# Loads placed ahead, and the heads' stores and small norm transfers moved from SyncE's queue to GpSimd's, in a hybrid SSD layer

## The chip, the cores and the metric

The kernel runs on one core of one Trainium2 chip. The metric is device microseconds of one execution. The core's engines are TensorE (PE, matmuls), VectorE (DVE), ScalarE (ACT), GpSimd (POOL) and SyncE (SP, which here only issues transfers); each works through its own list of instructions in order, and they wait for each other by semaphores. Times before the change: 1659.56, 1663.52 and 1663.94 us, median 1663.52.

## The reference, cut to what matters

One layer on a sequence of 2048 tokens of width 1024, fp32. `rmsnorm`, `silu`, `softplus` and the causal convolution `causal_dwconv` are as usual.

```python
h = rmsnorm(x, norm_pre)
xbc, dt_raw, z_ssd, sc_h, sc_b, sc_c, z_sc = split(h @ w_in)
xbc = silu(causal_dwconv(xbc, ssd_conv_w, ssd_conv_b))        # xs, bm, cm
dt, a = softplus(dt_raw + dt_bias), -exp(a_log)
# ssd_chunked: 16 heads of 64, 2 groups, state 64, chunks of 128
cb      = einsum("bclgn,bcsgn->bgcls", cc, bc)
y_diag  = einsum("bgrcls,bcsgrp->bclgrp", cb * decay_in, xd)
states  = einsum("bclgn,bclgrp->bcgrpn", bc, xd * decay_states)
# prev_states: states carried over the chunks, zero ahead of the first
y_off   = einsum("bclgn,bcgrpn->bclgrp", cc, prev_states) * decay_out
y       = y_diag + y_off + d_skip * xs
y_ssd   = grouped_rmsnorm(y * silu(z_ssd), ssd_norm)           # 2 groups
y_sc    = sc_b * causal_dwconv(sc_c * sc_h, sc_conv_w) * silu(z_sc)
x = x + rmsnorm(concat(y_ssd, y_sc) @ w_out, norm_post)
return x + sigmoid(x @ w_ple_gate) * (p @ w_ple_proj)
```

## The kernel before

All large products run as three matmuls of fp32 values that are split into a rounded half and its remainder (ACT casts, DVE subtracts). The input projection and the last gate product use seven sub-products (Strassen-Winograd). The sequence is cut in two blocks b of 1024 tokens and four groups of 512.

The stages, by the profile: to 50 us the per-layer embeddings; 50 to 570 the input projection of block 0, 570 to 1030 that of block 1; to about 1306 the heads; then the output projection (tiles `mo`) to about 1490, and the gate product (`mg`) to 1653.

*Under block 1's projection* `later_weights()` makes split halves of later weights: it loads rows `A_g` and `A_o`, and `keep` casts (ACT, L542), subtracts (DVE, L543) and stores them (SP, L544) to `sg_d` and `so_d`. Among ACT's other work there are copies of the projection's sums out of PSUM (L326), which free banks for PE.

*The heads* go in pairs j = 0 to 3 for each block. A pair loads xs, the rows `m` of accumulated decay (L1035) and the gate rows gz; ACT makes exponentials of m (L1003 for `ea`, L1040 for the mask m), DVE multiplies m with the products `gsb` (L1043), carries the states `sprev` from chunk to chunk (L1027) and forms `ea` (L1030); PE adds, in `py`, ea times sprev and m times xd. The result is gated on DVE (L1071, L1072) and stored to `yz_d` (L1073), and its squares are summed in `ssum`. `begin()` and `step_g` do what a block needs once: loads of `ct` and `bt` (L944, L946), their product (`pg`), which ACT copies to `gsb` (L961) and GpSimd masks (L963, the page's AFFINE_SELECT).

Between the heads' steps PE works on a filler, `under()`: the half of the output projection that reads the short convolution's rows (`os`, L817). Its sums go through `po` (ACT, L918) to `part_d` (SP, L919). The filler also makes the split rows of coming token groups: loads `mraw`, casts (L215) and subtracts (L216).

After a block's last pair `inv_rms` makes the group norm: a matmul over ssum (`pn`), a copy (L244), four stores of a row to `grs_d` (L246), a load of them in columns, `pn_q` (L249), a square root and a reciprocal (L251), and a store back (L252). The broadcast load `gn` of this (L856) is then used to make the rows of the output projection.

In the output projection DVE's L1180 adds a sum `mo` in PSUM to the stored part (load `part`), into `x2`; the second norm's small transfers are at L1200 and L1202. `second(tg, unit, at, lag)` adds the residual rows `xres`, which are loaded `lag` units before.

What sets the order: a scheduler places each engine's instructions at build time by its own cost estimates; matmuls of the heads and the filler stay in program order. Every transfer waits for the eighth before it of its kind of queue. Tiles come from pools that are opened and closed like a stack: a tile in a pool that lies where a closed pool lay waits for all that used that place.

## Time and profile before

| | |
|---|---|
| runs | 1659.56, 1663.52, 1663.94 us, median 1663.52 |
| profiled execution, own time | 1660.71 us |
| its span, first to last instruction | 1659.0 us |
| mean granted TensorE clock | 0.997 |
| PE busy | 1634.0 us (98%) |
| DVE, ACT, POOL busy | 1273.4 (77%), 805.7 (49%), 69.3 us (4%) |
| transfers | 314.73 MB, all of the program's issued on SP |

PE's busy time counts from the modelled start to the modelled end of a matmul. A line of a timeline gives a start, a duration, the engine and line, and a number of like instructions; in brackets stands how long the engine was idle before and what ended that. For a transfer, the time is that of its issue on SP (SPq), not of the data.

### The profile page before, as it was taken

How to read it: one execution, taken by the hardware profiler on the slowest of the kernel's cores; microseconds unless marked ns; L12 is line 12 of the kernel's file. 1: busy time of each engine (PE TensorE's matmuls, PEld its weight loads, DVE VectorE, ACT ScalarE, POOL GpSimd, SP SyncE). 2: the span in 40 equal slices, each digit the busy share in tenths (PEclk: the TensorE clock that was granted, in tenths of full speed). 3: DMA queues.
4: the chain of work that ended last, by engine and by line, in shares of the span. 5: the costliest groups of instructions: out<-in, count | busy, mean ns of one | idle time of the engine just before them, and what ended most of it. 6: DMA issues, size and time to landing. Idle time of an engine off the chain costs nothing.

```text
span 1659.0 us, 22821 instructions
## 1 busy us (share of the span) xinstructions
PE 1634.0 (98%) x8296; PEld 1344.2 (81%) x8296; DVE 1273.4 (77%) x1913; ACT 805.7 (49%) x1450; POOL 69.3 (4%) x79
## 2 busy tenths in 40 slices
PE   9999999999999999999999999999999999999998
PEld 8888888888888888788888888888788788888776
DVE  6998777987769999877768678478777747687785
ACT  8663444434337555543435345466667424234342
POOL 0000000000000311000000001000100000000000
PEclk9999999999999999999999999999999999999999
DMA  9352322774216478951323227788788635547996
GB/s 324 140 197 83 101 94 82 258 242 142 72 64 219 178 269 283 298 172 64 108 64 107 71 66 266 254 303 292 278 288 293 202 113 180 160 160 253 323 309 218
DMA packets 135557, 314.73 MB, mean 190 GB/s; under 512 B 18698, under 2 KB 20234, under 8 KB 135444
## 3 DMA queue, kind: packets, MB, share of 16 engines
q1 hardware_dynamic: 135444, 313.27, 55.3%
q8 instruction: 65, 1.06, 0.3%
q14 instruction: 48, 0.39, 0.1%
HBM read 221.81 MB, written 91.41 MB: 189 GB/s over the span
## 4 chain that ended last, share of the span: by engine, by line
PE 74%; DVE 10%; DMA 9%; ACT 4%; issue 2%; SPq 0%; DVEq 0%; ACTq 0%
PE mo L226 10%; PE mg_X L1278 4%; PE mg_Y L1278 4%; PE os L817 3%; PE A_ple L226 2%; DMA m<-acs_d 2%; ACT m L1040 1%; PE A_xs1X L322 1%; PE A_gc6X L322 1%; PE A_gb7X L322 1%; PE A_gb5X L322 1%; PE A_gc7X L322 1%; PE A_z3X L322 1%; PE A_xs3X L322 1%; PE A_gb6X L322 1%
## 5 line engine op out<-in xcount | busy, mean ns | idle before, releaser
L817 PE MATMUL os<-act_m,ws_os 128*128 128x512 f32 x768 | 184.6, 397 | 0.7 <-ACT A_z L749 0.7
L226 PE MATMUL mo<-act_m,ws_o 128*128 128x512 f32 x768 | 179.3, 394 | 3.5 <-DVE x L1180 3.3
L226 PEld LDWEIGHTS mo<-act_m,ws_o 128*128 128x128 f32 x768 | 144.0, 189 | 37.8 <-DVE x L1180 6.0
L817 PEld LDWEIGHTS os<-act_m,ws_os 128*128 128x128 f32 x768 | 142.9, 189 | 34.6 <-issue 4.2
L1278 PE MATMUL mg_X<-act_x2s,ws_g 128*128 128x512 f32 x384 | 90.8, 393 | 0.7 <-ACT gth L1249 0.7
L147 DVE TENSOR_TENSOR ws_A_gb<-wr_A_gb,ws_A_gb 128x512 fp32r<-128x512 f32 x96 | 65.7, 684 | 27.1 <-ACT ws_A_gb L146 27.1
L1278 PEld LDWEIGHTS mg_X<-act_x2s,ws_g 128*128 128x128 f32 x384 | 70.8, 188 | 18.6 <-ACT gth L1249 1.7
L146 ACT CAST ws_A_gc<-wr_A_gc 128x512 fp32r<-128x512 f32 x96 | 59.7, 622 | 49.7 <-PE A_gc5X L322 8.3
L146 ACT CAST ws_A_gb<-wr_A_gb 128x512 fp32r<-128x512 f32 x96 | 59.7, 622 | 48.4 <-issue 5.0
L668 DVE SCALAR_TENSOR_TENSOR xo<-ux,cols,xo 128x1024 f32<-128x1024 f32 x60 | 76.6, 1280 | 5.3 <-ACT xo L664 4.2
L1040 ACT ACTIVATE m<-m,adt 128x128 f32<-128x128 f32 x256 | 79.8, 390 | 0.5
L147 DVE TENSOR_TENSOR ws_A_gc<-wr_A_gc,ws_A_gc 128x512 fp32r<-128x512 f32 x96 | 65.8, 685 | 12.2 <-ACT ws_A_gc L146 11.4
L1278 PE MATMUL mg_Y<-act_x2s,ws_g 128*128 128x512 f32 x288 | 68.1, 392 | 1.7 <-DVE kp L1251 1.2
L1278 PEld LDWEIGHTS mg_Y<-act_x2s,ws_g 128*128 128x128 f32 x288 | 53.5, 188 | 14.7 <-DVE kp L1251 2.4
L1043 DVE SCALAR_TENSOR_TENSOR m<-m,gsb 128x1024 f32<-128x1024 f32 x32 | 39.5, 1247 | 28.2 <-ACT m L1040 20.0
L1180 DVE TENSOR_TENSOR x<-mo,part 128x512 f32<-128x512 f32 x32 | 22.1, 689 | 47.4 <-PE mo L226 42.4
L1185 ACT ACTIVATE sq<-x 128x512 f32<-128x512 f32 x28 | 17.7, 633 | 70.5 <-DVE x L1180 70.4
L146 ACT CAST ws_A_z<-wr_A_z 128x512 fp32r<-128x512 f32 x48 | 29.9, 623 | 40.9 <-DVE wr_A_z L199 13.9
L215 ACT CAST act_m<-mraw 128x512 fp32r<-128x512 f32 x64 | 37.5, 620 | 23.8 <-DMA mraw<-ysc_d 9.6
L146 ACT CAST ws_A_xs<-wr_A_xs 128x512 fp32r<-128x512 f32 x48 | 29.9, 623 | 36.6 <-issue 11.6
L226 PE MATMUL A_ple<-act_p,ws_p 128*128 128x512 f32 x192 | 45.8, 396 | 0.1
L147 DVE TENSOR_TENSOR ws_A_z<-wr_A_z,ws_A_z 128x512 fp32r<-128x512 f32 x48 | 32.9, 685 | 16.6 <-ACT ws_A_z L146 16.5
(521 smaller groups left out, 3742.7 us busy)
## 6 DMA issues: line engine op xcount, KB each, us to landing
ws_g<-sg_d SPq DMA_DIRECT2D x56, 512.0 KB, 5.0
wr_A_gc<-in_w_t_dram SPq DMA_DIRECT2D x64, 256.0 KB, 2.7
wr_A_gb<-in_w_t_dram SPq DMA_DIRECT2D x64, 256.0 KB, 3.0
ws_os<-so_d SPq DMA_DIRECT2D x32, 512.0 KB, 5.7
m<-acs_d SPq DMA_DIRECT2D x32, 512.0 KB, 6.4
sg_d<-A_gs SPq DMA_DIRECT2D x28, 512.0 KB, 4.3
ple_d<-A_pe SPq DMA_DIRECT2D x32, 256.0 KB, 3.9
wr_A_xs<-in_w_t_dram SPq DMA_DIRECT2D x32, 256.0 KB, 3.0
```

Of the source, the lines that this page charges most:

```text
L146: S.copy(sp[:, 0, :kn, :], raw[:, :kn, :])
L147: V.tensor_tensor(sp[:, 1, :kn, :], raw[:, :kn, :], sp[:, 0, :kn, :].bitcast(F32), ALU.subtract)
L215: S.copy(a[:, 0, :], src)
L226: TE.matmul(out, sp[:, a, (k0 + k) % 4, :], act[k0 + k][:, b, :], start=k0 + k == 0 and q == 0, stop=k0 + k == n - 1 and q == 2)
L322: TE.matmul(out, sp[:, a, k % 4, :], t[:, b, ts_], start=p in OPENS and k == 0 and q == 0, stop=k == nk - 1 and q == 2, skip_group_check=True)
L668: V.scalar_tensor_tensor(o, u[:, q:q + TB], col(w0 + q), o, ALU.mult, ALU.add)
L817: inst = f(*a, **k)
L1040: S.activation(m[:, c, :], m[:, c, :], AF.Exp, bias=nacs[b][:, h, c:c + 1])
L1043: V.scalar_tensor_tensor(mf, mf, 1.0, s["gsb"][gr], ALU.min, ALU.mult)
L1180: evac.append(V.tensor_tensor(x2[d], ps[:, i, :], pt[:, i, :], ALU.add))
L1185: S.activation(sq, x2[d], AF.Square)
L1278: TE.matmul(out, sp[:, a, k, :], ops_[t, p][k][:, b, :], start=p in OPENS and m_ == 0, stop=m_ == 11, skip_group_check=True)
```

## The change

- `later_weights` issues the loads of A_o three ahead of the `keep` that uses them.
- GpSimd's queue, not SP's, issues the 32 stores to `part_d`, the 16 stores to `yz_d`, the heads' norms' small transfers (parameter `by` of `inv_rms`) and the second norms' store and broadcast load, 68 transfers in all.
- The first chunk's state is no longer written out: block 0 copies the first sums from PSUM and leaves out the products with the zero state, block 1 reads `carry` in place. GpSimd's memsets and copies go.
- The rows of token group 2 are loaded one at a time and earlier (`load_raw`, `mix_tile`), and the mixing of groups 3 and 0 is spaced otherwise.
- `ct`, `gsb` and `btok` get a pool of their own below `per`; x2's tiles get one (`px`) that is opened first, below the part loads. x2 so lies where the heads' working tiles (po and others, `t4`) lay, and the part loads where ct, gsb and btok lay.
- `second(2, ...)` and `second(3, ...)` get lags of 3 and 4 units, from 2.

```diff
-    def inv_rms(row_d, accs, eps, name, banks, scale=1.0):
+    def inv_rms(row_d, accs, eps, name, banks, scale=1.0, by=nc.sync):
-            nc.sync.dma_start(row_d.rearrange("a (g t) -> (a g) t", t=TG)[g:g + 1, :], row[32 * g:32 * g + 1, :])
+            by.dma_start(row_d.rearrange("a (g t) -> (a g) t", t=TG)[g:g + 1, :], row[32 * g:32 * g + 1, :])
-        nc.sync.dma_start(q, col_d)
+        by.dma_start(q, col_d)
-        nc.sync.dma_start(col_d, q)
+        by.dma_start(col_d, q)
...
-            for d in range(KD):
-                for q in range(2):
-                    w = A.ph.tile([P, TG], F32, tag="h2", name=f"A_o{d}_{q}")
-                    nc.sync.dma_start(w.rearrange("p (k c) -> p k c", c=P), w_o[d, :, 4 * (q + 2):4 * (q + 2) + 4, :])
-                    keep(so_d[d][q], w, f"A_os{d}_{q}")
+            ahead = []
+            for n in range(2 * KD + 3):
+                if n < 2 * KD:
+                    d, q = divmod(n, 2)
+                    ahead.append(A.ph.tile([P, TG], F32, tag="h2", name=f"A_o{d}_{q}"))
+                    nc.sync.dma_start(ahead[n].rearrange("p (k c) -> p k c", c=P),
+                                      w_o[d, :, 4 * (q + 2):4 * (q + 2) + 4, :])
+                if n >= 3:
+                    d, q = divmod(n - 3, 2)
+                    keep(so_d[d][q], ahead[n - 3], f"A_os{d}_{q}")
                     yield
...
+        pg_ = st.enter_context(tc.tile_pool(name="pg", bufs=1))
         per = st.enter_context(tc.tile_pool(name="per", bufs=1))
...
+            def load_raw(tg, k):
+                t = praw.tile([P, 4, P], F32, tag="wraw", name=f"mraw_{tg}_{KD + k}").rearrange("p k c -> p (k c)")
+                b, o = divmod(tg * TG, TB)
+                nc.sync.dma_start(t, ysc_d[b][k, :, o:o + TG])
+                raws[k] = t
...
-                            nc.sync.dma_start(part_d[tg][dp + di], o)
+                            G.dma_start(part_d[tg][dp + di], o)
...
-                    sp_ = st["sp"] = t4.tile([P, NCH, P], F32, tag="sprev", name=f"sprev_{b}{j}", bufs=1)
+                    sp_ = t4.tile([P, NCH, P], F32, tag="sprev", name=f"sprev_{b}{j}", bufs=1)
                     ea = st["ea"]
-                    if b == 0:
-                        G.memset(sp_[:, 0, :], 0.0)
-                    else:
-                        G.tensor_copy(sp_[:, 0, :], carry[:, j, :])
+                    prev = st["prev"] = [carry[:, j, :] if b else None] + [sp_[:, c, :] for c in range(1, NCH)]
...
+                        if prev[c] is None:
+                            V.tensor_copy(dstn, pst[:, :P])
+                            continue
...
-                    for c in range(NCH):
+                    for c in range(0 if b else 1, NCH):
...
-                    nc.sync.dma_start(yz_d[b][jt], yv)
+                    G.dma_start(yz_d[b][jt], yv)
...
-                        epsc[:, 1:2], f"pn_{b}", ssd_bank, scale=2.0)
+                        epsc[:, 1:2], f"pn_{b}", ssd_bank, scale=2.0, by=G)
...
+        px = st.enter_context(tc.tile_pool(name="px", bufs=NG * KD + 4))
+        L3 = Loads(st, "pl3", 3)
         pp = st.enter_context(tc.tile_pool(name="pp", bufs=2))
-        L3 = Loads(st, "pl3", 3)
...
-                nc.sync.dma_start(rs2_d[tg].rearrange("a (p c) -> (a p) c", c=TG // P), q)
+                G.dma_start(rs2_d[tg].rearrange("a (p c) -> (a p) c", c=TG // P), q)
...
-                nc.sync.dma_start(rs, rs2_d[tg].partition_broadcast(P))
+                G.dma_start(rs, rs2_d[tg].partition_broadcast(P))
...
-        second(2, 32, (40, 41, 43, 44), 2)
+        second(2, 32, (40, 41, 43, 44), 3)
...
-        second(3, 36, (56, 58, 60, 61), 2)
+        second(3, 36, (56, 58, 60, 61), 4)
```

How the order of the instructions moves at three places follows; the line numbers are each kernel's own, and the last number of a name tells apart buffers.

ACT in block 1's projection, at the copies of the sums cb0 (`A_1_cb0_1` and `A_1_cb0_5`), before and then after:

```order
L727 ACTIVATE vs_12_5952<-us_12_5948,cols_108 128x1024
L749 COPY A_z0_12_5971<-A_1_gb2X_5695 128x512
L146 CAST ws_A1_cb0_2_0_5987<-wr_A1_cb0_010_5931 128x512
L699 ACTIVATE th_120_5973<-A_z0_12_5971 128x512
L326 COPY A_1_cb0_1_6002<-A_1_cb0X_5986 128x512
L146 CAST ws_A1_cb0_4_0_6005<-wr_A1_cb0_110_5888 128x512
L542 CAST A_os6_1_7367<-A_o6_1_7365 128x512
L542 CAST A_os7_0_7410<-A_o7_0_7408 128x512
L542 CAST A_os7_1_7472<-A_o7_1_7470 128x512
L326 COPY A_1_cb0_5_6020<-A_1_cb0Z_6004 128x512
```

```order
L542 CAST A_os6_1_7371<-A_o6_1_7245 128x512
L146 CAST ws_A1_cb0_7_0_5956<-wr_A1_cb0_100_5886 128x512
L732 ACTIVATE vs_12_5952<-us_12_5948,cols_108 128x1024
L542 CAST A_os7_0_7412<-A_o7_0_7290 128x512
L754 COPY A_z0_12_5971<-A_1_gb2X_5695 128x512
L146 CAST ws_A1_cb0_2_0_5987<-wr_A1_cb0_010_5931 128x512
L704 ACTIVATE th_120_5973<-A_z0_12_5971 128x512
L542 CAST A_os7_1_7472<-A_o7_1_7330 128x512
L326 COPY A_1_cb0_1_6002<-A_1_cb0X_5986 128x512
L146 CAST ws_A1_cb0_4_0_6005<-wr_A1_cb0_110_5888 128x512
L326 COPY A_1_cb0_5_6020<-A_1_cb0Z_6004 128x512
```

The three casts that stood together ahead of the second copy now stand apart and earlier; the last stands ahead of the first copy. On SP the loads of A_o6_1 and A_o7_0 now stand ahead of two loads wr_A1_gc3 that wait for DVE, and that of A_o7_1 behind them, where all three stood.

SP at the second pair of block 0, before and then after:

```order
L980 DMA xs_05_9016<-xs_d0_72 128x1024
L919 DMA part_d0_78<-po_0_2_9036 128x512
L1035 DMA m_02_9163<-acs_d0_94 128x1024
L1035 DMA m_03_9165<-acs_d0_94 128x1024
L1073 DMA yz_d0_69<-xs_00_8751 128x1024
L919 DMA part_d0_78<-po_0_3_9156 128x512
L1073 DMA yz_d0_69<-xs_04_8753 128x1024
L1035 DMA m_010_9167<-acs_d0_94 128x1024
L1035 DMA m_011_9169<-acs_d0_94 128x1024
L1007 DMA gz_01_9209<-gz_d0_74 128x1024
```

```order
L1013 DMA xs_05_9017<-xs_d0_72 128x1024
L154 DMA ws_os0_4_1_8954<-so_d4_100 128x1024
L913 DMA mraw_2_15_9833<-ysc_d1_83 128x512
L142 DMA wr_o0_0_0_11179<-in_w_o_dram 128x512
L1069 DMA m_02_9160<-acs_d0_94 128x1024
L1069 DMA m_03_9162<-acs_d0_94 128x1024
L1069 DMA m_010_9164<-acs_d0_94 128x1024
L1069 DMA m_011_9166<-acs_d0_94 128x1024
L1040 DMA gz_01_9206<-gz_d0_74 128x1024
```

The two stores of xs and the part stores between the loads of m are gone from SP; the four loads stand together, as they do at every later pair.

The end of the heads. PE at the start of the output projection, before and then after (`mo_0_0` is the first sum; its second bank starts with `ws_o0_1_0` and waits for the first x2 out of the first bank):

```order
L226 MATMUL mo_0_0_11530<-act_m_0_7_11432,ws_o0_0_1_11200 128x512 x3
L226 MATMUL mo_1_0_11609<-act_m_1_0_11494,ws_o0_0_0_11195 128x512 x3
L226 MATMUL mo_1_0_11609<-act_m_1_1_11497,ws_o0_0_0_11195 128x512 x3
L226 MATMUL mo_1_0_11609<-act_m_1_2_11500,ws_o0_0_0_11195 128x512 x3
L226 MATMUL mo_1_0_11609<-act_m_1_3_11503,ws_o0_0_0_11195 128x512 x3
L226 MATMUL mo_1_0_11609<-act_m_1_4_11506,ws_o0_0_1_11200 128x512 x3
L226 MATMUL mo_1_0_11609<-act_m_1_5_11509,ws_o0_0_1_11200 128x512 x2
L226 MATMUL mo_0_0_11530<-act_m_0_0_11383,ws_o0_1_0_11533 128x512 x3
```

```order
L226 MATMUL mo_0_0_11517<-act_m_0_7_11435,ws_o0_0_1_11183 128x512 x3
L226 MATMUL mo_1_0_11596<-act_m_1_0_11477,ws_o0_0_0_11178 128x512 x3
L226 MATMUL mo_1_0_11596<-act_m_1_1_11480,ws_o0_0_0_11178 128x512
L226 MATMUL mo_0_0_11517<-act_m_0_0_11360,ws_o0_1_0_11520 128x512 x3
L226 MATMUL mo_0_0_11517<-act_m_0_1_11364,ws_o0_1_0_11520 128x512 x3
```

And POOL there after the change (before, POOL issues nothing):

```order
L1107 DMA yz_d1_70<-xs_17_10889 128x1024
L942 DMA part_d3_81<-po_3_6_11407 128x512
L246 DMA grs_d1_87<-ssum_10_10077 16x1x32 x4
L942 DMA part_d3_81<-po_3_7_11470 128x512
L249 DMA pn_1_q_11459<-grs_d1_87 128x16
L252 DMA grs_d1_87<-pn_1_q_11459 128x16
```

The wait for the first x2 now comes after 28 matmuls of mo, where it came after 41; the last part store stands behind the four stores of the norm. At the first norm POOL's order is the same with two more rows: the masks of gsb_10 and gsb_11 stand between the load of pn_q and the store back.

More of the change, by code (lines that the diff above doesn't have):

```diff
@@ L900, in under @@
                     pieces = []
+                    if dp == KD - 2:
+                        if t == 0:
+                            new += [lambda k=k: load_raw(2, k) for k in range(KD)]
+                        else:
+                            new += [no] * 10 + [lambda: mix_load(L, 0, 0), lambda: mix_load(L, 0, 2)]
                     for tg in (t, t + 1):
@@ L918, in under @@
                             S.copy(o, ps)
-                            nc.sync.dma_start(part_d[tg][dp + di], o)
+                            G.dma_start(part_d[tg][dp + di], o)
                         if dp == KD - 2 and tg < NG - 1:
-                            new += mixes(*((tg + 2, KD) if tg + 2 < NG else (tg + 2 - NG, 0)))
+                            ld = lambda tg, k: lambda: mix_load(L, tg, k)
+                            mx = lambda tg, k: lambda: mix_pair(L, tg, k)
+                            if tg == 0:
+                                for k in range(KD):
+                                    new.append(lambda k=k: mix_tile(raws, 2, k))
+                                    if k in (2, 4, 6):
+                                        ld(3, KD + k - 2)()
+                            elif tg == 1:
+                                new += [mx(3, KD), ld(3, KD + 6), no, mx(3, KD + 2), no, mx(3, KD + 4), no, no, mx(3, KD + 6)]
+                            else:
+                                new += [mx(0, 0), ld(0, 4), no, mx(0, 2), ld(0, 6), no, no, no, mx(0, 4), no, no, mx(0, 6)]
         late = {}
@@ L942, in begin @@
             def begin():
-                s["ct"] = per.tile([P, TB], F32, tag="ct", name=f"ct_{b}")
+                s["ct"] = pg_.tile([P, TB], F32, tag="ct", name=f"ct_{b}")
                 nc.sync.dma_start(s["ct"], cb_d[b][0])
@@ L946, in begin @@
                 nc.sync.dma_start(s["bt"], cb_d[b][1])
-                s["gsb"] = [per.tile([P, TB], F32, tag=f"gsb{gr}", name=f"gsb_{b}{gr}") for gr in range(2)]
-                s["btok"] = per.tile([P, NCH, P], F32, tag="btok", name=f"btok_{b}")
+                s["gsb"] = [pg_.tile([P, TB], F32, tag=f"gsb{gr}", name=f"gsb_{b}{gr}") for gr in range(2)]
+                s["btok"] = pg_.tile([P, NCH, P], F32, tag="btok", name=f"btok_{b}")
                 s["ssum"] = [per.tile([P, TB], F32, tag=f"ssum{gr}", name=f"ssum_{b}{gr}") for gr in range(2)]
```

16 lines of the change are left out of this document (9 added, 7 removed).

## The prediction

> **What bounds the kernel now.** I read the waits of TensorE (PE) first, then a table of stretches, then the timelines around each long wait. The profiled execution's span is 1659.0 us and its own time 1660.71; the median of the runs shown is 1663.52, 2.8 above it, so the sum is made as a difference and taken off the median. PE is busy 98%, so the change can win little more than PE's idle time. Columns: engine, line, who releases it, us in total, times, longest.
>
> ```profile
> PE A_cb0Z L322 <- ACT A_cb L326: 3.6, 1, 3.6
> PE mo L226 <- DVE x L1180: 3.3, 1, 3.3
> PE py L817 <- DVE ea L1030: 3.2, 5, 0.8
> PE pn L817 <- DVE ssum L1078: 2.7, 2, 2.3
> PE mg_Y L1278 <- DVE kp L1251: 1.2, 1, 1.2
> ...
> PE pg L817 <- DMA bt<-cb_d: 1.1, 1, 1.1
> ```
>
> These six make 15.1 us. A gap costs more than itself where the granted clock drops behind it (columns: stretch, its length, busy us of PE, weight loads, DVE, ACT, POOL, then the clock, DMA share, GB/s):
>
> ```profile
> 1065.00:1300.00 235.00, 227.43 (x2047) 188.98 (x2044) 180.47 (x271) 145.95 (x328) 7.53 (x9) 0.99 0.77 275
> 1160.00:1180.00 20.00, 17.31 (x120) 12.76 (x116) 18.02 (x20) 12.23 (x22) 3.61 (x1) 0.91 0.87 319
> 1320.00:1340.00 20.00, 20.00 (x83) 15.94 (x83) 8.66 (x13) 3.92 (x7) 0.00 (x0) 0.94 0.66 211
> ```
>
> The heads' stage (first row) idles 235 - 227.4 = 7.6 us on PE. A clock of 0.91 over 20 us is 1.8 us lost behind the pn gap, 0.94 is 1.2 behind the mo gap. All that is in reach is so about 18 us; what SP waits for its stores costs nothing of itself unless a load that stands behind ends a PE wait.
>
> **Part 1: A_o rows loaded ahead.** The largest wait is near 700 us (start, duration, engine, line, operation, count, idle before and releaser):
>
> ```profile
> 699.74 2.89 PE L322 MATMUL A_cb0X<-act_A,ws_A_cb 128*128 128x512 f32 x12
> 706.20 0.96 PE L322 MATMUL A_cb0Z<-act_A,ws_A_cb 128*128 128x512 f32 x3 [3.57 <-ACT A_cb L326]
> ...
> 703.23 1.35 ACT L542 CAST A_os<-A_o 128x512 fp32r<-128x512 f32 x2 [3.21 <-DMA A_o<-in_w_o_dram]
> 705.04 0.62 ACT L542 CAST A_os<-A_o 128x512 fp32r<-128x512 f32 x1 [0.47 <-DMA A_o<-in_w_o_dram]
> 705.57 0.58 ACT L326 COPY A_cb<-A_cb0Z 128x512 f32<-128x512 f32 x1
> ...
> 695.74 1.53 SPq L142 DMA_DIRECT2D wr_A_gc<-in_w_t_dram  x2
> 697.32 1.37 SPq L565 DMA_DIRECT2D A_o<-in_w_o_dram  x3
> ```
>
> ACT's copy of A_cb0Z frees the bank that PE wants, and stands behind three A_os casts whose rows were issued only at 697.32, behind two wr_A_gc loads. After the change two of the three rows stand ahead of those loads; the last, A_o7_1, still stands behind both. Its issue falls between 695.5 (loads released a little sooner, as ACT no longer waits for earlier rows) and 697.3. But the last cast now stands ahead of the A_cb copy of the product before, so PE is caught at 699.74 and not at 702.63. From a middle issue of 696.2 and a landing of 4 us, against some 6 in the rows above (703.23 - 697.32), as one row and not three is in flight: 700.2, cast 0.6 and copy 0.6 to 701.4, so PE waits 1.6 instead of 3.57. I take **+2.0** (gain positive throughout). Ends: the whole wait, +3.6; or issue at 697.3 and 6.3 us, copy done at 704.8, wait 5.1, -1.5.
>
> **Part 2: no matmuls against the zero state.** 64 of these take 1.98 us:
>
> ```profile
> 1199.27 1.98 PE L817 MATMUL py<-ea,sprev 64*64 64x128 f32 x64
> ```
>
> Each b=0 pair drops 8 of its 64: 4 x 8 x 31 ns = **+1.0**. The POOL memset and copies that go were off the path; the copy on DVE replaces two of 0.27 us and leaves the chain to ea a shade shorter. Ends 0.5 and 1.1.
>
> **Part 3: SP freed of 48 stores and the norms' transfers.** Before, the exponent rows m are loaded in pieces, held by stores whose data is late:
>
> ```profile
> 1076.34 0.80 SPq L1035 DMA_DIRECT2D m<-acs_d  x2
> 1078.96 0.32 SPq L1073 DMA_DIRECT2D yz_d<-xs  x1
> ...
> 1082.18 1.59 SPq L1035 DMA_DIRECT2D m<-acs_d  x2
> ...
> 1088.63 1.06 ACT L1003 ACTIVATE ea<-m 64x1024 f32<-64x1024 f32 x1 [1.01 <-DMA m<-acs_d]
> ...
> 1092.53 1.23 DVE L1043 SCALAR_TENSOR_TENSOR m<-m,gsb 128x1024 f32<-128x1024 f32 x1 [4.83 <-ACT m L1040]
> ...
> 1100.45 0.43 PE L817 MATMUL py<-ea,sprev 64*64 64x128 f32 x4 [0.58 <-DVE ea L1030]
> 1101.49 1.96 PE L817 MATMUL py<-ea,sprev 64*64 64x128 f32 x60 [0.61 <-DVE ea L1030]
> ```
>
> The last two m go out at 1082.18, wait 6.4 us for data, ACT idles 1.01 for them, DVE waits 4.83 for ACT, then runs its chain to ea, and PE waits 1.19. With four m in a row they go out at 1077.1, five earlier; but ACT is nearly full here, so what comes forward is about that 1.01. Of the 3.2 us of five such waits I take **+2.0** (ends 0 and 3.2). The bt load has the same cause:
>
> ```profile
> 1172.92 0.88 SPq L946 DMA_DIRECT2D bt<-cb_d  x1
> ...
> 1178.37 1.11 SPq L246 DMA_DIRECT2D grs_d<-ssum  x4
> ...
> 1181.77 0.32 SPq L249 DMA_DIRECT2D pn_q<-grs_d  x1
> ...
> 1186.69 2.14 POOL L963 TENSOR_SCALAR_AFFINE_SELECT gsb<-gsb 128x1024 f32<-128x1024 f32 x2 [23.08 <-ACT gsb L961]
> ...
> 1187.82 4.36 DVE L1043 SCALAR_TENSOR_TENSOR m<-m,gsb 128x1024 f32<-128x1024 f32 x3 [7.06 <-POOL gsb L963]
> ```
>
> Without the store of xs ahead of it, bt goes out some 2 us sooner: the 1.1 us of pg goes, **+1.0** (ends 0 and 1.1). The pn gap stays, **0**: VectorE's own chain of sums ends it, and VectorE is busy 18.02 of 20 us there. Two xd products now come before the last sum, one wait on ACT less; ends -2 and +2.
>
> What this puts on POOL is the unknown: before, POOL issues no DMA at all. A DMA's issue costs SP 0.28 us (1.11 for four) and is the nearest row; POOL's own full-tile operation, the select, takes 1.07 each, and I bound the issue by 0.28 and 2 us, the second the two selects together. At the first norm POOL now does four grs stores, a part store and the pn_q load (which waits there, in order, for the stores' landing) before the two selects for which DVE waits to 1187.82. From 1178.37 with 1 us each: four to 1182.4, landed 2.3 later (SP's pn_q went out 2.3 after its last store), pn_q issued by 1185.7, ahead of the 1186.69 at which the selects start anyway: **0**. At 2 us each, 1178.4 + 8 + 2.3 + 2 = 1190.7, the selects start 4.0 late, and DVE, py and PE with them.
>
> **Part 4: the pools, and the end of the heads.** The mo gap:
>
> ```profile
> 1306.40 9.46 PE L226 MATMUL mo<-act_m,ws_o 128*128 128x512 f32 x41
> 1319.19 5.16 PE L226 MATMUL mo<-act_m,ws_o 128*128 128x512 f32 x15 [3.33 <-DVE x L1180]
> ...
> 1308.30 1.12 SPq L246 DMA_DIRECT2D grs_d<-ssum  x4
> 1309.82 0.34 SPq L919 DMA_DIRECT2D part_d<-po  x1
> ...
> 1313.61 1.40 SPq L856 DMA_DIRECT2D part<-part_d  x3
> ...
> 1311.94 1.89 DVE L147 TENSOR_TENSOR ws_o<-wr_o,ws_o 128x512 fp32r<-128x512 f32 x3
> 1318.45 0.69 DVE L1180 TENSOR_TENSOR x<-mo,part 128x512 f32<-128x512 f32 x1 [4.62 <-DMA part<-part_d]
> ...
> part_d<-po SPq DMA_DIRECT2D x27, 256.0 KB, 4.3
> ```
>
> The first x waits for the part load, issued at 1313.61 behind the norm's small transfers. After the change that load's slot and queue are free early. But x's own tile lies where the po tiles were: it waits for the last part store, which now stands on POOL behind four grs stores that start at 1308.30; and PE's order now meets x after 28 matmuls (1306.4 + 6.4 = 1312.8), not 41. With 0.28 us an issue the store goes out by 1309.8, lands 4.3 later at 1314.1, DVE (busy to 1313.83) ends x at 1314.8: a gap of 2.0, +1.3. With 1 us each it goes out at 1313.3, lands at 1317.6, x ends at 1318.3: 5.5, -2.2. I take the middle, **0**, near which the ends balance. The xres loads one or two units earlier can take some of mg_Y's 1.2: **+0.5** (ends 0 and 1.2).
>
> Sum: 2.0 + 1.0 + 2.0 + 1.0 + 0 + 0 + 0.5 = 6.5 us; 1663.5 - 6.5 = **1657.0**.
>
> A rule speaks against the change. The Trainium skill, DMA: Bandwidth & Descriptors, section SWDGE vs HWDGE vs iDMA, says that GpSimd builds its descriptors in software where SP's are made in hardware; the section on one DMA's anatomy gives about 2.0 us fixed per transfer. No row of this trace shows it; by an estimate from that figure the store at the mo gap would land no later than by the rows here, so the sum stands.
>
> **The rivals.**
> (a) *GpSimd is held while VectorE runs.* Two rows of the same tile at the same places (busy us, mean ns):
>
> ```profile
> L720 POOL COPY us<-halo_s 128x2 f32<-128x2 f32 x8 | 26.2, 3274 | 260.6 <-DVE xo L670 207.9 <-DVE A_z L700 49.6 <-DVE vs L729 3.1
> ...
> L718 POOL MEMSET us<- 128x2 f32 x8 | 0.8, 100 | 138.3 <-DVE xo L670 124.0 <-DVE A_z L700 14.3
> ```
>
> A copy of two columns takes 3.27 us, a memset of them 0.1: POOL is held when it reads. If its DMA issue is held in the same way, nothing goes out while DVE runs back to back to 1313.83; five issues of 1 us then bring the last store to 1318.8, its landing to 1323.1 and x to 1323.8: a gap of 11.0, 7.7 more than now and about 2 more of clock. At the first norm DVE is free after 1180.8: four stores to 1184.8, landed 1187.1, pn_q to 1188.1, the selects 1.4 late. And the xs loads now wait for yz stores that are held as well, which I let take 1.5 of the 2.0 at py. 6.5 - 7.7 - 2 - 1.4 - 1.5 = -6.1: **1669.6**, slower. It decides from about 2 us per issue on at mo. Against: the memsets are not held.
> The Trainium skill, SBUF — State Buffer, section Who interferes with whom, has it that a VectorE instruction with two SBUF inputs contends with a GpSimd instruction that reads SBUF, not with one that only writes. The trace agrees (3274 against 100 ns); whether a DMA's issue counts as a read no run here shows.
> (b) *The loads were hidden anyway.* ACT or DVE bounds each chain, PE meets the A_cb copy one product sooner, and only the dropped matmuls and a part of bt are left: +2, **1661.5**. For it: DVE is busy 18.0 of 20 us at the pn gap, and at py it waits 4.83 us for ACT's exponents while ACT itself waits only 1.01 for data.
> (c) *The early part load closes the mo gap too.* POOL issues as fast as SP and DVE's chain shortens: +3.3 + 1.2 of clock there, +3.2 at py, the full 3.6: 3.6 + 1.0 + 3.2 + 1.1 + 4.5 = 13.4, less what DVE's own work still holds of mo, 1.7: **1652**.
>
> **How the numbers follow.** Forecast 0.50, (a) 0.17, (b) 0.20, (c) 0.13. A change within 0.3%, 5 us, can't be told from none. The forecast's own range, 1653 to 1661, lies some two thirds below 1658.5: 0.50 x 0.7 + 0.13 = 0.48 faster; 0.50 x 0.3 + 0.20 x 0.9 = 0.33 same; the rest slower, 0.19. The range takes in (c) and, at its upper end, (a): 1648 to 1670.
>
> **What would show it.** A_cb0Z's wait falls below 2 and is named at the product before; py<-ea,sprev counts 480; py's waits fall to about 1 us and pg's is gone; m goes out in fours. POOL's issue, once seen, decides between the forecast and (a): near 1 us or less, the selects still start by 1187; the mo wait moves to after 28 matmuls, and its length says which end held. The forecast is wrong if stores on POOL land late enough to hold the xs loads, which now wait for yz stores, or if a new wait on PE above 2 us appears in the heads.

## The result and the profile after

The change made the kernel slower: a median of 1678.77 us (1676.95 to 1680.64) against 1663.05 for the kernel before, run beside it (1659.56 to 1663.94), a ratio of 1.0085 with a 95% interval of 1.0061 to 1.0109. The forecast of 1657.0 had the wrong sign, and 1678.77 lies above its range. The profiled execution took 1680.64 us over a span of 1678.9, 19.9 more than the span before; the medians differ by 15.7, since the execution that was profiled before was 2.3 below its median and the one after 1.9 above. What follows explains the spans.

TensorE's waits after (columns as in the prediction):

```profile
PE A_cb0X L322 <- ACT A_cb L326: 7.3, 1, 7.3
PE py L822 <- DVE ea L1064: 7.0, 12, 2.1
PE mo L226 <- DVE x L1214: 5.7, 1, 5.7
PE pn L822 <- DVE ssum L1112: 5.4, 1, 5.4
PE mg_Y L1312 <- DVE x L1244: 1.5, 1, 1.5
PE mg_Y L1312 <- DMA ws_g<-sg_d: 1.2, 1, 1.2
```

The same four places lead the list, each longer than before: 28.1 us in these six rows against 15.1. Only pg's wait is gone. Behind the three long gaps, and behind the longest wait at py, the clock falls (the table of stretches, after; the clock is the third figure from the end):

```profile
700.00:720.00 20.00, 12.74 (x44) 9.96 (x43) 12.92 (x22) 7.48 (x17) 3.87 (x5) 0.74 0.83 281
1180.00:1200.00 20.00, 15.50 (x89) 11.18 (x91) 9.91 (x11) 16.89 (x34) 5.21 (x8) 0.83 0.71 276
1240.00:1260.00 20.00, 20.00 (x190) 17.34 (x190) 13.74 (x12) 10.06 (x19) 1.76 (x4) 0.92 0.68 239
1320.00:1340.00 20.00, 14.25 (x54) 11.06 (x51) 10.79 (x18) 8.86 (x16) 3.63 (x7) 0.83 0.30 86
```

Busy time times the missing clock is 3.3 + 2.6 + 1.6 + 2.4 = 9.9 us in these, against 17.31 x 0.09 + 20 x 0.06 = 2.8 in the two stretches that the prediction showed. The page's totals agree: TensorE idles 38.3 us of the span where it idled 25.0, of which the six rows are 13.0, and is busy 1640.6 us where it was busy 1634.0, though it runs 32 matmuls fewer; 13.3 + 6.6 are the 19.9. The slower clock (7.1 by these stretches), less some 0.8 for the dropped matmuls, makes 6.3 of the 6.6. Where the time came, by the first matmul of a stage:

| first matmul of | before | after | later by |
|---|---|---|---|
| the sums A_dt, behind cb0 | 717.21 | 724.71 | 7.5 |
| pn, the first norm | 1171.02 | 1177.95 | 6.9 |
| mo, the output projection | 1306.40 | 1321.84 | 15.4 |
| mg, the gate product | 1486.34 | 1504.89 | 18.6 |
| end of the span | 1659.0 | 1678.9 | 19.9 |

**cb0.** The timelines of SP, VectorE, ScalarE and TensorE after:

```profile
700.75 0.33 SPq L142 DMA_DIRECT2D wr_A_gc<-in_w_t_dram  x1
701.13 0.45 SPq L567 DMA_DIRECT2D A_o<-in_w_o_dram  x1
...
700.04 0.68 DVE L147 TENSOR_TENSOR ws_A_cb<-wr_A_cb,ws_A_cb 128x512 fp32r<-128x512 f32 x1
...
706.94 0.62 ACT L542 CAST A_os<-A_o 128x512 fp32r<-128x512 f32 x1 [3.58 <-DMA A_o<-in_w_o_dram]
707.46 0.58 ACT L326 COPY A_cb<-A_cb0X 128x512 f32<-128x512 f32 x1
...
708.09 5.49 PE L322 MATMUL A_cb0X<-act_A,ws_A_cb 128*128 128x512 f32 x12 [7.26 <-ACT A_cb L326]
```

The last row A_o was issued at 701.13, not at 695.5 to 697.3 as the prediction has it. It stands behind a wr_A_gc load, which went out when a VectorE subtract ended (700.04 + 0.68). That subtract is itself late because ScalarE, which feeds it, waits for the earlier A_o rows: the loads and the casts go round in a ring (as the timelines are read here), and ScalarE's whole wait for A_o rose from 11.8 us in seven times to 18.6 in nine. The copy that frees PE's bank stands behind the last cast. After 7.26 us of idle time twelve matmuls took 5.49 us where they took 2.89.

**The heads.** The worst of the twelve py waits, block 1's second pair:

```profile
1213.21 2.54 SPq L1069 DMA_DIRECT2D m<-acs_d  x4
...
1219.40 1.06 ACT L1036 ACTIVATE ea<-m 64x1024 f32<-64x1024 f32 x1 [2.30 <-DMA m<-acs_d]
...
1228.55 1.23 DVE L1077 SCALAR_TENSOR_TENSOR m<-m,gsb 128x1024 f32<-128x1024 f32 x1 [5.09 <-ACT m L1074]
1231.37 1.23 DVE L1077 SCALAR_TENSOR_TENSOR m<-m,gsb 128x1024 f32<-128x1024 f32 x1 [1.59 <-ACT m L1074]
1233.71 1.23 DVE L1077 SCALAR_TENSOR_TENSOR m<-m,gsb 128x1024 f32<-128x1024 f32 x1 [1.12 <-ACT m L1074]
1234.85 0.47 DVE L1061 SCALAR_TENSOR_TENSOR sprev<-carry,ea,pst 128x64 f32<-128x64 f32 x2
...
1227.78 1.97 PE L822 MATMUL pst<-xdd,btok 128*64 128x128 f32 x32
...
1238.90 0.44 PE L822 MATMUL py<-ea,carry 64*64 64x128 f32 x4 [2.13 <-DVE ea L1064]
```

The four m do go out together, as forecast. But VectorE's list has three mask products (m times gsb) ahead of the chain that PE waits for, the states `sprev` and `ea`. Each mask product waits for ScalarE's exponentials. The last input of the states, the sums pst, is ready at 1229.75, and the chain starts at 1234.85, behind two masks that came after. At this pair there were two ahead before; counted over the eight pairs, in the order of the program, 22 before and 23 after. So the placement is an old fault of the schedule. Over the heads VectorE's waits for ScalarE's m grew from 20.0 us in 11 times to 24.8 in 16, and ScalarE's for m ahead of ea from 9.2 to 20.5 (2.30 of it here). Whether the third mask or the later data cost more at this pair was not separated.

**The first norm, pn:**

```profile
1166.91 4.04 SPq L142 DMA_DIRECT2D wr_o<-in_w_o_dram  x4
1171.04 2.20 SPq L1069 DMA_DIRECT2D m<-acs_d  x4
...
1179.38 1.06 ACT L1036 ACTIVATE ea<-m 64x1024 f32<-64x1024 f32 x1 [3.85 <-DMA m<-acs_d]
...
1182.10 1.04 ACT L1111 ACTIVATE gz<-xs 128x1024 f32<-128x1024 f32 x1
...
1183.17 1.23 DVE L1112 TENSOR_TENSOR ssum<-ssum,gz 128x1024 f32<-128x1024 f32 x1 [3.46 <-ACT gz L1111]
...
1184.45 1.92 PE L822 MATMUL pn<-ssum,ones_d 128*32 128x512 f32 x4 [5.45 <-DVE ssum L1112]
```

ScalarE's order was gz, ea, gz, ea before and is gz, ea, ea, gz now. The last square of the old block stands behind two ea of the next (the second, at 1180.85, waited 0.41 more), whose m were issued only at 1171.04, behind four wr_o loads.

**mo:**

```profile
1322.49 3.37 ACT L215 CAST act_m<-mraw 128x512 fp32r<-128x512 f32 x6 [2.22 <-DVE mraw L877]
1325.77 0.57 ACT L244 COPY ssum<-pn 128x512 f32<-128x512 f32 x1
...
1326.73 2.05 POOL L246 DMA_DIRECT2D grs_d<-ssum  x4 [7.06 <-ACT ssum L244]
1328.99 0.58 POOL L942 DMA_DIRECT2D part_d<-po  x1 [0.21 <-ACT ws_o L146]
...
1323.04 5.50 DVE L216 TENSOR_TENSOR act_m<-mraw,act_m 128x512 fp32r<-128x512 f32 x9
...
1333.35 0.69 DVE L1214 TENSOR_TENSOR x<-mo,part 128x512 f32<-128x512 f32 x1 [1.80 <-issue]
```

PE meets x after the 28 matmuls that started at 1321.84, and the last part store goes out behind the four grs stores, as the prediction has it; it landed 4.1 us after 1328.99, at 1333.1, and x started at 1333.35 (the trace itself names no releaser for x). New is that the norm's copy (L244) comes 3.9 us after the first mo, where it came 1.3 after it (1307.69 against 1306.40): behind ScalarE's last wait for VectorE six casts of act_m stand ahead of it, not three, and they start 0.65 us behind the first mo, not 0.42 ahead of it.

### The profile page after: what moved, and what is told of

Read it like the earlier page. It is cut to its first block, busy times and chain, and to the rows that moved or that the text cites. A ratio compares the mean times of both kernels' runs of the same rounds, so it can differ in the third digit from the quotient of the medians.

```text
span 1678.9 us, 22772 instructions
## 1 busy us (share of the span) xinstructions
PE 1640.6 (98%) x8264; PEld 1347.2 (80%) x8264; DVE 1275.3 (76%) x1909; ACT 805.1 (48%) x1450; POOL 99.7 (6%) x139
## 5 line engine op out<-in xcount | busy, mean ns | idle before, releaser
L147 DVE TENSOR_TENSOR ws_A_gc<-wr_A_gc,ws_A_gc 128x512 fp32r<-128x512 f32 x96 | 66.0, 687 | 12.1 <-ACT ws_A_gc L146 11.2
L1312 PEld LDWEIGHTS mg_Y<-act_x2s,ws_g 128*128 128x128 f32 x288 | 53.5, 188 | 15.6 <-issue 1.9
L1077 DVE SCALAR_TENSOR_TENSOR m<-m,gsb 128x1024 f32<-128x1024 f32 x32 | 39.8, 1250 | 32.2 <-ACT m L1074 24.8
L1219 ACT ACTIVATE sq<-x 128x512 f32<-128x512 f32 x28 | 17.7, 633 | 70.2 <-DVE x L1214 70.1
```

What stands on the lines that cost most here:

```text
L147: V.tensor_tensor(sp[:, 1, :kn, :], raw[:, :kn, :], sp[:, 0, :kn, :].bitcast(F32), ALU.subtract)
L1077: V.scalar_tensor_tensor(mf, mf, 1.0, s["gsb"][gr], ALU.min, ALU.mult)
L1219: S.activation(sq, x2[d], AF.Square)
L1312: TE.matmul(out, sp[:, a, k, :], ops_[t, p][k][:, b, :], start=p in OPENS and m_ == 0, stop=m_ == 11, skip_group_check=True)
```

## The experiments

All ratios are to the kernel before, run on the same chip beside them, with 95% intervals. Names of parts are those of the diff above.

### The A_o rows

**e1_rows** is the kernel before with the new loop of `later_weights` alone.

```diff
+                if n >= 3:
+                    d, q = divmod(n - 3, 2)
+                    keep(so_d[d][q], ahead[n - 3], f"A_os{d}_{q}")
```

> The kernel before with one part of the change, the loads of A_o three ahead. Theory (in the trace after the change PE's wait at cb0 grew from 3.6 to 7.3 us and the matmuls behind it ran slower, A_dt starting 6.6 us later): this part loses 6 to 7 us by itself, wait of PE named at A_cb0X near 7 us, time about 1669.5. Rival (the wait grew because other parts moved the order of that stage): wait near 3.6 or less, time 1660 to 1664.

1669.13 us, 1.0015 (1.0003 to 1.0027). PE's wait is 6.3 us at A_cb0X, and ScalarE waits 17.7 us for A_o rows. Alone this part costs some 2.5 us, where +2.0 was forecast as a gain; the wait came as expected, but not a loss of 6 to 7 us, and the time near 1669.5 was met only because the kernel before, beside it, had a median of 1665.43.

**e12_rows_pool**: the same, its loads issued by GpSimd, and so not behind SP's wr loads.

```diff
-                    nc.sync.dma_start(ahead[n].rearrange("p (k c) -> p k c", c=P),
+                    G.dma_start(ahead[n].rearrange("p (k c) -> p k c", c=P),
```

> The kernel before with A_o's loads three ahead and issued by GpSimd's queue. Theory (A_o's rows were late because on SP they stand behind loads that wait for VectorE, which waits for the casts of those rows): ScalarE's waits for A_o go, PE's wait at cb0 falls from 3.6 (before) and 6.3 (three ahead on SP) to under 1 us, 2 to 4 us faster than before. Rival (rows by this queue land late as the stores did): the wait stays at 3 us or more.

1672.54, 1.0032 (1.0011 to 1.0053). The expectation failed: ScalarE still waits 15.6 us for A_o, and PE's one long wait has become three, 3.0 and 2.3 at A_cb0X and 2.8 at A_gc2X. Taking the rows off SP's queue doesn't bring them in time: GpSimd's issues of A_o wait 25.7 us in five times for VectorE's subtracts of earlier rows.

**e15_copies**: the kernel before, with each cast of A_os bound behind the last copy that the program has ahead of it. No load is written otherwise, but the binding moves the whole of this work. The casts in the kernel before and in this one (shortest, median and longest in ns, then the first and the last start):

```profile
L542 ACT CAST A_os<-A_o x16: 616/620/627, 650.1 to 705.0; 128x512 fp32r<-128x512 f32 x16
L542 ACT CAST A_os<-A_o x16: 616/621/626, 780.5 to 858.3; 128x512 fp32r<-128x512 f32 x16
```

```diff
-                        S.copy(keep[pr, p], out)
+                        self.copied = S.copy(keep[pr, p], out)
...
+                if name.startswith("A_os"):
+                    tc.add_manual_dep(cast.ins, A.copied.ins.name, NOSYNC, reason="after the copy")
```

> The kernel before with the casts of A_o forced behind the copies of the projection's sums that the program has ahead of them (they then run in a later part of block 1). Theory (a cast that waits for its row stands ahead of the copy that frees PE's bank): the wait at cb0, 3 to 3.6 us, goes altogether, and the time is 3 to 4 us shorter. Rival (the copy waits for something else, or the later casts make a wait of their own): a wait of 2 us or more at cb0 or at os.

1659.03, 0.9971 (0.9956 to 0.9985). ScalarE's timeline at the place, in this kernel:

```profile
699.46 0.59 ACT L326 COPY A_cb<-A_cb0X 128x512 f32<-128x512 f32 x1 [1.08 <-PE A_cb0X L322]
...
702.18 0.59 ACT L326 COPY A_cb<-A_cb0Z 128x512 f32<-128x512 f32 x1 [1.61 <-PE A_cb0Z L322]
```

The copies now wait for PE, and PE is busy for all of 640 to 720 us. So what held the bank were the casts ahead of the copies, as ScalarE's timeline before shows. But the run does more than swap them: with the A_o work gone to a later part of block 1, the DMA share of 640 to 720 us falls from 0.90 to 0.44. What the order alone would do, with the casts still in this stretch, no run shows.

**e18_rows_copies**: the rows ahead with that order.

```diff
+                    keep(so_d[d][q], ahead[n - 3], f"A_os{d}_{q}")
...
+                    tc.add_manual_dep(cast.ins, A.copied.ins.name, NOSYNC, reason="after the copy")
```

> The A_o rows loaded ahead, alone, with the casts forced behind the copies. If the cast ahead of the copy is what costs, and not the loads' places, the wait at cb0 goes as it does with the order alone, and the time is that of the order alone, 0.996 to 0.998. If the rows ahead add something of themselves (SP or the bank in use for longer), 1.000 or more; if they bring something once the order is right, below 0.995.

1658.84, 0.9969 (0.9954 to 0.9984): the time of e15_copies. Here too the casts run late, at 778.3 to 856.0. Once they are there, loading ahead adds nothing and costs nothing.

### The stores and the norms' transfers

**e2_queue** moves all 68 transfers to GpSimd and changes nothing else; **e4_no_rows** is the whole change without the rows ahead; **e3_rest** is the pools, lags, mixing and zero state alone, with every transfer on SP.

```diff
-                            nc.sync.dma_start(part_d[tg][dp + di], o)
+                            G.dma_start(part_d[tg][dp + di], o)
-                    nc.sync.dma_start(yz_d[b][jt], yv)
+                    G.dma_start(yz_d[b][jt], yv)
-                        epsc[:, 1:2], f"pn_{b}", ssd_bank, scale=2.0)
+                        epsc[:, 1:2], f"pn_{b}", ssd_bank, scale=2.0, by=G)
-                nc.sync.dma_start(rs2_d[tg].rearrange("a (p c) -> (a p) c", c=TG // P), q)
+                G.dma_start(rs2_d[tg].rearrange("a (p c) -> (a p) c", c=TG // P), q)
```

> The kernel before with the 68 transfers issued by GpSimd's queue, and nothing else. Theory (stores on this queue land later: yz_d 8.3 us in place of 4.0, and SP's xs loads, which wait for them, hold the loads of m behind them): 7 to 12 us slower, 1670 to 1675, with SP waiting over 20 us in all at the xs loads for yz_d stores. Rival (the loads of output weights and single rows, which the change puts ahead of the loads of m, are the cause): 1660 to 1665.

> The changed kernel with A_o's loads as before. Theory: the changed kernel's time less 6 to 7, about 1672, the wait at cb0 back at 3.6 us. Rival (the gap is refilled elsewhere): within 3 us of the changed kernel, 1676 to 1680.

> The changed kernel with A_o's loads as before and all transfers on SP: the zero state left out, the rows of group 2 loaded singly, the pools and the lags. Theory: the dropped matmuls (1 us) and the pools give a little, 1659 to 1663. Rival (the moved loads are the cause): 1670 to 1675.

e2_queue 1671.76, 1.0038 (1.0022 to 1.0053), with waits of 6.5 at mo, 6.1 at pn and 5.1 at py; e4_no_rows 1674.78, 1.0054 (1.0038 to 1.0071), with py 9.4, mo 6.9, pn 5.1; e3_rest 1665.08, 0.9994 (0.9980 to 1.0008). The larger part of the loss comes with the moved transfers. The rest is worth nothing that can be told from none, though it drops 32 matmuls and 1659 to 1663 us were expected. The parts do not add up: rows, transfers and rest make 1.0015, 1.0038 and 0.9994, some 0.0047 together, and the whole change 0.0085. The missing 6 us, little more than the noise of four ratios, appear only when the parts stand together, and no run shows why.

**e5_stores** moves the part and yz stores only, **e7_yz** and **e8_part** one kind each, **e6_norms** the heads' norms' transfers alone.

```diff
+                            G.dma_start(part_d[tg][dp + di], o)      # e5_stores, e8_part
+                    G.dma_start(yz_d[b][jt], yv)                     # e5_stores, e7_yz
+                        epsc[:, 1:2], f"pn_{b}", ssd_bank, scale=2.0, by=G)   # e6_norms
```

> The kernel before with only the 48 stores (part_d and yz_d) by GpSimd's queue; the norms' transfers stay on SP. Theory (xs loads on SP wait for yz_d stores that land in 8 us, and m waits behind them): py and pn keep their longer waits, 5 to 6 us each, and the mo wait falls back to about 3 to 4 since the last part store no longer stands behind four norm stores; 1668 to 1671 on this scale, where the kernel before had 1665.4. Rival (GpSimd's norm transfers are the cause): 1664 to 1667.

> The kernel before with only the 16 yz_d stores by GpSimd's queue. Theory: these carry the larger part of the queue's loss: yz_d lands in 7 to 8 us, SP waits 20 us or more for it at the xs loads, 3 to 5 us slower. Rival (the landing is long only when all 48 stores crowd one queue): yz_d lands in 4 to 5 us and the time stays within 2 us.

> The kernel before with only the 32 part_d stores by GpSimd's queue. Theory: nothing on SP waits for these before the output projection, so SP is freed of some 70 us of waits and the py waits fall from 3.2 to about 2: 0 to 2 us faster. Rival (any store on this queue costs): 2 to 4 us slower.

> The kernel before with only the heads' norms' small transfers by GpSimd's queue. Theory: no loss, within 2 us of the kernel before, the selects start as before, since an issue on GpSimd took 0.5 us in the changed kernel. Rival (the norm's transfers on GpSimd are the cause): 3 us or more slower, with the wait at pn or mo up by 3.

| | us | ratio | PE's waits at py, pn, mo |
|---|---|---|---|
| e5_stores | 1674.47 | 1.0065 (1.0041 to 1.0089) | 6.6, 5.8, 5.2 |
| e7_yz | 1671.62 | 1.0051 (1.0032 to 1.0070) | 5.8, 4.2, 5.2 |
| e8_part | 1669.54 | 1.0032 (1.0018 to 1.0046) | 5.5, 2.3, 4.8 |
| e6_norms | 1667.29 | 1.0021 (1.0010 to 1.0033) | 3.4, 2.6, 4.0 |

Each costs by itself, e8_part too, of which a small gain was expected, and e6_norms, of which none of this was; its one new wait is 2.1 us at pst, for ScalarE's copy of btok. In e5_stores the mo wait did not fall to 3 or 4 us either, and e7_yz lost more than the 3 to 5 us expected. The three single parts add to 0.0104, far above the 0.0038 of e2_queue, which moves them all and the second norms' transfers too: every edit gets a new order on every engine, and a part's own cost cannot be read from one run. The 16 yz stores cost most, and land 7.3 us after issue where they landed in 4.0. That spoke for the late landing as the cause: the xs loads wait for these stores.

**e9_act** tests that: the same two kinds of stores issued by ScalarE's queue.

```diff
+                            nc.scalar.dma_start(part_d[tg][dp + di], o)
...
+                    nc.scalar.dma_start(yz_d[b][jt], yv)
```

> The kernel before with the 48 stores issued by ScalarE's queue, right behind the ScalarE work that makes or reads the data. Theory (GpSimd's queue delivers stores late whatever the moment): yz_d lands in 4 to 5 us as on SP, SP waits for it under 10 us in all at the xs loads, and the time is within 3 us of the kernel before. Rival (any store that goes out when its data is ready meets the loads that SP then issues): yz_d lands in 7 to 8 us here too and the time is 8 to 11 us longer, as with GpSimd's queue.

1653.0, 0.9931 (0.9905 to 0.9958): faster than before. Its transfers between 1030 and 1340 us (queue, count, KB, median us to landing):

```profile
part_d<-po ACTq DMA_DIRECT2D x32, 256.0 KB, 5.2
yz_d<-xs ACTq DMA_DIRECT2D x16, 512.0 KB, 8.0
```

and those of the changed kernel in the same stretch:

```profile
part_d<-po POOLq DMA_DIRECT2D x32, 256.0 KB, 4.9
yz_d<-xs POOLq DMA_DIRECT2D x16, 512.0 KB, 8.3
```

The stores land as late as on GpSimd, and SP waits for yz stores as long (34.2 us at the xs loads against 35.8). Yet py's wait is 1.1, pn's 1.7 and mo's 0.4. So neither the landing nor SP's wait for it makes the loss, and that theory falls. What differs is the order that the scheduler made: masks ahead of the states are 9 over the eight pairs (as 3,1,1,1 and 0,1,1,1; in the fifth pair one more stands behind the first state), where e5_stores has 22 and the change 23, and ScalarE's order at pn is ea, gz, gz. Neither of the two expectations saw a gain coming.

### VectorE's order

**e10_order** is the kernel before with three of a pair's four mask products bound behind the states and ea; **e11_after_order** is the change with the same; **e13_pool_order** is e5_stores with it and **e14_act_order** e9_act with it.

```diff
-                        V.scalar_tensor_tensor(ea[:, hh, :], s["ct"], 0.5, ea[:, hh, :], ALU.mult, ALU.mult)
+                        st["last"] = V.scalar_tensor_tensor(ea[:, hh, :], s["ct"], 0.5, ea[:, hh, :], ALU.mult, ALU.mult)
-                    V.scalar_tensor_tensor(mf, mf, 1.0, s["gsb"][gr], ALU.min, ALU.mult)
+                    inst = V.scalar_tensor_tensor(mf, mf, 1.0, s["gsb"][gr], ALU.min, ALU.mult)
+                    if "last" in st:
+                        tc.add_manual_dep(inst.ins, st["last"].ins.name, NOSYNC, reason="states first")
```

> The kernel before with one thing forced in VectorE's order: the second to fourth mask product of a pair (L1043) come behind the states and ea, as the program has them, where the scheduler put two or three of them ahead. Theory (py waits for ea because a mask product that waits for ScalarE's exponents stands ahead of the states): py's waits fall from 3.2 to under 1 us, 2 to 4 us faster. Rival (the states wait for pst, or ea for the last loads of m): py's waits stay above 2.5.

> The changed kernel with the same order forced. Theory: py's waits fall from 7 to 2 us or less and the time by 4 to 7 us, so that this order, and not the landing of m alone, made the loss in block 1's pairs. Rival (the loads of m land too late for ea itself): py's waits stay above 5 us.

> The kernel before with the 48 stores by GpSimd's queue and the states forced ahead of the mask products on VectorE. Theory (the queue lost time through the order: the same waits, met with masks ahead of the states): py's waits under 1 us, and the time within 3 us of the kernel before with the order alone (0.9955 of before), so 0.993 to 0.998. Rival (GpSimd's queue costs something of its own): 1.001 or more of before.

> The kernel before with the 48 stores by ScalarE's queue and the same order forced. Theory (with ScalarE's queue the scheduler already put one mask or none ahead of the states in all pairs but the first, so it won by the order): little more than the stores by ScalarE alone (0.9931), 0.990 to 0.994. Rival (its gain is the queue's and adds to the order's 0.9955): 0.989 or less.

| | us | ratio |
|---|---|---|
| e10_order | 1658.04 | 0.9955 (0.9938 to 0.9972) |
| e11_after_order | 1667.35 | 1.0015 (0.9998 to 1.0033) |
| e13_pool_order | 1660.31 | 0.9974 (0.9957 to 0.9990) |
| e14_act_order | 1652.02 | 0.9934 (0.9914 to 0.9953) |

PE's two longest waits in e11_after_order:

```profile
PE A_cb0X L322 <- ACT A_cb L326: 7.4, 1, 7.4
PE mo L226 <- DVE x L1216: 6.2, 2, 6.0
```

py falls from 7.0 to 0.3 in the change and from 3.2 to nothing in the kernel before, though the yz stores of e11_after_order land in 8.1 us. In e10_order VectorE's waits for ScalarE's m fall from 20.0 us to 0.3. Its gain of some 7.5 us is more than expected and more than its profile shows: idle time is 4.3 us less than before, but PE's busy time in that execution is 3.9 us more, at a clock of 0.994; where the rest of the median's gain lies was not found. With the order forced, the stores on GpSimd are 0.9974, not 1.0065; on ScalarE nothing moves (0.9934 against 0.9931), as the scheduler had placed them so already. The two queues still differ by 8.3 us (9.2 in the profiled spans: 5.0 of idle time and 4.2 of longer busy time). The rows at mo differ by 4.7 and those at pn by 2.7; at mo SP's order explains it. In e13_pool_order:

```profile
1306.54 1.12 SPq L246 DMA_DIRECT2D grs_d<-ssum  x4
1311.27 0.36 SPq L142 DMA_DIRECT2D wr_o<-in_w_o_dram  x1
1311.83 0.35 SPq L249 DMA_DIRECT2D pn_q<-grs_d  x1
1312.60 1.39 SPq L856 DMA_DIRECT2D part<-part_d  x3
```

and in e14_act_order:

```profile
1302.36 1.12 SPq L246 DMA_DIRECT2D grs_d<-ssum  x4
1304.38 0.35 SPq L249 DMA_DIRECT2D pn_q<-grs_d  x1
1304.90 1.40 SPq L856 DMA_DIRECT2D part<-part_d  x3
```

In the first a wr_o load, which waited 3.5 us for VectorE and is late at 1311.27, stands ahead of pn_q and of the part loads for which x waits (3.71); in the second it stands behind them. Why the scheduler placed these otherwise was not measured, nor what GpSimd's queue would cost with one and the same order on every engine.

### Both bindings, and a faster version

**e17_after_both** is the change with both bindings.

```diff
+                        tc.add_manual_dep(inst.ins, st["last"].ins.name, NOSYNC, reason="states first")
...
+                    tc.add_manual_dep(cast.ins, A.copied.ins.name, NOSYNC, reason="after the copy")
```

> The change with both orders forced: the masks behind the states, as in the run before, and the A_os casts behind the copies that the program has ahead of them. If the two orders are what turned the change into a loss, the 7.4 us at A_cb0X (and about 1 to 2 of clock behind it) go, the 0.3 at py stay: 1667 less 8 is about 1659, 0.995 to 0.998 of the kernel before, with mo at about 6 and pn at 3 left over. If the moved stores or loads cost something of themselves that no order mends, it stays at 1665 or more.

1657.07, 0.9962 (0.9950 to 0.9973). Its two longest waits:

```profile
PE mo L226 <- DVE x L1218: 6.0, 2, 5.8
PE pn L824 <- DVE ssum L1116: 3.1, 1, 3.1
```

Two bindings, each a few lines, turn 1.0085 into 0.9962 (the second moves the A_o work as in e15_copies: its casts run at 778.5 to 856.2). This does not make the change a gain: the same bindings on the kernel before, each alone, gave 0.9955 and 0.9971. If they add up, which no run tried, they come to 0.9926 together, and the change then costs 0.0036, about 6 us, of which mo's longer gap is 2.5 (5.8 against 3.33).

**e16_act_copies** takes what was of use: the part and yz stores by ScalarE's queue, the casts behind the copies, no zero state, and the lags of `second`.

```diff
+                            nc.scalar.dma_start(part_d[tg][dp + di], o)
+                    nc.scalar.dma_start(yz_d[b][jt], yv)
+                    tc.add_manual_dep(cast.ins, A.copied.ins.name, NOSYNC, reason="after the copy")
```

> Stores by ScalarE's queue, the casts behind the copies, and of the change the zero state and the lags. Theory: the gains add: 0.9931, less 3 to 5 us at cb0 (5.7 us of waits there with ScalarE's queue), less 1 us of matmuls: 0.988 to 0.991 of before. Rival (the parts' orders disturb each other, as in the change): 0.993 or more.

1646.15 us, 0.9898 (0.9880 to 0.9917), as expected: faster than both kernels. Its longest waits are 3.4 us in two times at pn and 1.6 at mg_Y, and the clock is 0.999 over the span.

## Why the prediction was wrong, point by point

By its own terms, in us of the profiled executions (gains positive):

| step | forecast | measured |
|---|---|---|
| Part 1, cb0 | +2.0 (-1.5 to 3.6) | -3.7 idle, and some 3 of clock |
| Part 2, dropped matmuls | +1.0 | +0.8 |
| Part 3, py | +2.0 (0 to 3.2) | -3.8 |
| Part 3, bt and pg | +1.0 | +1.1 |
| Part 3, pn | 0 (-2 to 2) | -2.7 |
| Part 3, GpSimd at the first norm | 0 | under 0.3 lost, counted at py |
| Part 4, mo | 0 (-2.2 to 1.3) | -2.4, and some clock |
| Part 4, lags | +0.5 (0 to 1.2) | -1.0 |

- **Part 1** failed at "its issue falls between 695.5 and 697.3". The step "loads released a little sooner, as ACT no longer waits for earlier rows" was wrong: ScalarE waited longer for them, so SP's loads came later, to 701.13. That the wait would be met one product sooner was right, and this made it worse. The clock behind the gap was left out of the bounds, though the prediction had shown it at pn and mo. By the runs the part costs some 2.5 us added to the kernel before (e1_rows) and some 5 taken from the change (1.0085 less the 1.0054 of e4_no_rows).
- **Part 2** was right: TensorE's count falls from 8296 to 8264, and a pair's row of 52 matmuls of py takes 1.75 us where one of 60 took 1.96: 4 x 0.21 = 0.8.
- **Part 3, py**, failed at "what comes forward is about that 1.01". The prediction read, in a quoted row, VectorE's wait of 4.83 us for ScalarE ahead of a mask product, and took the mask for a step of the chain to ea. It is none: the masks only stand ahead of it. e10_order shows this, since taking them out of the way removes py's wait in the kernel before, with the same transfers on SP's queue, in an order that differs at a few places. At the pair that the prediction worked out the waits did fall, from 1.19 us to 0.61, and the four m went out together; but it took one pair for all, and most other pairs lost, block 1's second most: 2.74 us where it had 1.41.
- **Part 3, bt**: right, the pg row is gone, but in part by luck: bt went out 3.5 us sooner as counted from PE's first pn, took 11.2 us to land where it took 8.0, and PE came to pg 3.1 us later for its longer gap at pn.
- **Part 3, pn**, failed at "one wait on ACT less": the wait on ScalarE for the last square grew to 3.46, because ScalarE's list now has two ea in front of it. The prediction looked at VectorE's rows there and not at ScalarE's. No run changes this order by itself; with VectorE's order forced (e11_after_order) 3.1 us are left at pn, with the stores on GpSimd and that order (e13_pool_order) 4.9, so the cause there is read from the timelines only.
- **GpSimd's issue** lies within the bounds, at 0.49 to 0.56 us (below). The selects started at 1195.55, right behind pn_q's issue and some 0.6 us after ScalarE had the first gsb ready; PE's wait at the py that follows is 0.26. The zero held.
- **Part 4, mo**: the mechanism was right and a size was off. Store behind store on GpSimd, met after 28 matmuls: all as written. With 0.54 us an issue its sum would give a gap of about 3. What was mis-sized in the sum is the start of the grs stores, taken as 1.9 us behind the first mo and measured as 4.9.
- **The lags** brought nothing at mg_Y: 2.7 us in its two rows against 1.7 (the 1.2 shown and a row of 0.5). Of the 2.7, 1.2 is a wait for a load of ws_g; no run has the lags alone.

Of the rivals, (a) fell with GpSimd's issue times, though its time was the nearest; (b) and (c) fell with the sign. Both of the prediction's signs of failure came: a wait above 2 us in the heads (2.13 at py), and stores that land late and hold the xs loads (35.8 us). But the second is not what made the loss: e9_act has the same late stores and is faster.

## What to carry to other kernels

Where a scheduler orders each engine's list, a moved transfer is first of all a new order: before costing the transfer, read in each waiting engine's list what stands ahead of the instruction that ends the wait, and whether that needs to stand there. An instruction whose data comes late, ahead of one that PE waits for, was the costliest thing here; binding the order in one or two places (e10_order, e15_copies) was a smaller edit than moving loads, and here a surer one. Look at what a binding moves: that of e15_copies shifted sixteen casts by some 130 us. Costs of parts, each measured alone, need not add up where every edit is scheduled anew. Try a transfer's other possible issuers too: the same 48 stores were 1.0065 on one queue and 0.9931 on another.
